# A decoder trunk on one core: the first down group's weights prepared block by block, the statistics' transpose in another PSUM bank, and the merge's low parts on Pool

## The chip, the cores and the metric

The kernel runs on one core of a Trainium2 chip. Its engines work side by side, each through its own queue of instructions in a fixed order: TensorE (PE in the profile) does the matrix products, with a weight load (PEld) ahead of each matmul; VectorE (DVE) and ScalarE (ACT) do elementwise work; GpSimd (POOL) does a little of it; SyncE (SP) issues the DMAs. Matmul results land in PSUM, all other tiles lie in SBUF. An engine waits at an instruction until the semaphores it needs have been raised, and what is queued behind it waits too.

The metric is device time in microseconds, the median over several executions.

## The reference

Two layers of a decoder trunk on 1024 tokens of width 1024, then a last RMSNorm. In each layer:

```
h = rmsnorm(x, norm1)
proj = h @ w_in                      # q, k, v of two mixers, and two gates
o_a = dilated_mixture(...)           # 3 groups x 4 heads, sliding windows, combined by their softmax denominators
o_b = stick_breaking_attention(...)  # 4 heads
merged = sigmoid(gate_a) * (o_a @ w_br[:256]) + sigmoid(gate_b) * (o_b @ w_br[256:])
x = x + merged @ w_o
up = rmsnorm(x, norm2) @ w_up        # 2 x 2816 columns: a gate half and a value half
a = causal_depthwise_conv(a, conv_w, conv_b)   # 3 taps
x = x + (gelu(a) * v) @ w_down
```

All inputs and outputs are float32.

## The kernel before, in words

**Products.** A float32 product is made of three matmuls in a reduced format: every operand is split into a high part `hi` (a cast) and a low part `lo` (the difference), and hi x hi, hi x lo and lo x hi are summed in PSUM. The helper `split` does it: ACT casts (L141), DVE subtracts (L148). `piece` does the same into a ring of four weight slots (tags `wh` and `wl`). One tile is 128 partitions x 512 columns, and most elementwise instructions handle one tile.

**Seven products.** The up chunks and the down-projection use a scheme of the Strassen kind: a product of 2 x 2 blocks is made of seven block products, each of which takes a sum or difference of weight blocks, made on DVE, and of inputs, and adds into one or more outputs.

**The up stage.** An up chunk (`up(j)`) is one unit of a chain. A unit's work is emitted in pieces; at its beginning and at each of its "turns" (five in an up chunk) the next unit is moved on by one piece, so that it can load and prepare its first weights while this one still multiplies. The convolution of a chunk (ACT L1468, DVE L1470 and L1471, ACT's Gelu L1473) and its gating (L1496) come after its last products. The gated result `g` is split, written to DRAM as `gd`, and read back as `gd_in` for the down-projection.

**The down stage.** `down(box)` is the last unit of the chain. It has 28 steps: four groups (of 2, 2, 3 and 4 row blocks of w_down) times the seven products k = 0 to 6. Step s multiplies one weight tile per row block i (two of them in the first group) with `gd_in`, into four PSUM banks e = 0 to 3 (L1759 to L1761, each block 3 matmuls per bank), and adds each bank to x on DVE (L1767). Steps 0 to 3 of a group use the same four banks, so the first matmul of s=1 in bank e waits for the add of bank e from s=0. `prep` prepares the weights of a step: for k=0 the difference a11 - a21 into `wd_s` (L1730, needed later) and the split of a11; for k=1 a sum in place (L1733), a difference in place (L1734) and the split; for k=6 a difference in place (L1737). In the last up chunk's turns, the unit loads the two raw blocks (`wd_raw`) and the inputs of two steps, and at the fifth turn calls `prep(0, 1)`: the weights of s=0, block 0 and then block 1. Those of s=1 are prepared by `prep(0)` when the down stage itself begins.

**The statistics' transpose.** In the near part of the first mixer, when the last item of a pair of heads has been folded, a 128 x 32 tile of softmax statistics is transposed by PE into a PSUM bank (`st0_t`), copied out by ACT (`st_r`, L842) and written to DRAM. PSUM has eight banks in four tags of two ("t", "o", "s", "ps"); the transpose takes one of tag "t", as do the transposes of the attention weights (`t1`, L921 to L923), whose results ACT and DVE split into `p1h` and `p1l` for the products into `o1` (L931, L933).

**The merge stage.** Sixteen items (two halves n of the tokens, eight column blocks e) a layer. An item is two products on PE into two banks `br_ps` (L182 to L184, 12 matmuls), two multiplications with the gates on DVE (L1416, `gin`), their sum on DVE (L1421, `mrg`), and one item later `merged`: ACT casts the high part `hh` (L1381), DVE subtracts the low part `hl` (L1382). DVE also makes the low parts of the branch weights `br_w` and of the first weights of the output projection here. The output projection (`o_ps`, L182 to L184 too) follows and reads `hh` and `hl` of all eight column blocks.

**What sets the order.** The instructions of each engine are ordered by a scheduler from the order of the code, its own estimates of durations, and priorities: what stands under `tc.high_priority(offset=AHEAD)`, such as the adds of L1767, is treated as if it had been written 200 instructions sooner.

Of the kernel before, what the change touches and what calls it, by code (L numbers as in the profile page):

```python
# [8 lines left out]
F32R = mybir.dt.float32r  # L9
# [3 lines left out]
ALU = mybir.AluOpType  # L13
# [3 lines left out]
P = 128  # L17
# [3 lines left out]
HF = 512  # L21
# [15 lines left out]
READY = 6  # L37
# [19 lines left out]
def f32(ap):  # L57
    return ap.bitcast(F32)
# [3 lines left out]
def trunk_kernel(ctx, tc, x, norm1, w_in, b_gate, w_br, w_o, norm2, w_up, conv_w, conv_b, w_down, norm_f, out, depth=None, probe=None):  # L62
# [62 lines left out]
    def bank(tag, name):  # L125
        return ps.tile([P, 512], F32, tag=tag, name=name)

    def small(name, dtype=F32):
        return sb.tile([P, 512], dtype, tag="pt", bufs=PT, name=name)
# [8 lines left out]
    def split(hi, lo, src, turn=None, behind=None):  # L138


        one = act.copy(hi, src)  # L141
        if behind:
            tc.add_manual_dep(one.ins, behind[0], NO_SYNC, reason="behind")
        if turn == "is":
            LAST["act"] = one.ins.name
        elif turn == "waits" and "act" in LAST:
            tc.add_manual_dep(one.ins, LAST["act"], NO_SYNC, reason="in turn")
        two = dve.tensor_tensor(lo, src, f32(hi), ALU.subtract)  # L148
        if behind:
            tc.add_manual_dep(two.ins, behind[1], NO_SYNC, reason="behind")  # L150
        if turn == "is":
            LAST["dve"] = two.ins.name
        return two
# [622 lines left out]
    def near_item(dense, pr, s):  # L776
        if s == 0:
            R["st0", pr] = sb.tile([P, 2, 2, 8], F32, tag="st0", bufs=2, name="st0")
        if "on" not in R:
            R["on"] = sb.tile([P, 2, T], F32, tag="xa", bufs=4, name="on")  # L780
        slot = 2 * pr + s
        q, kv, on, st = R["slots"], R["kvn", slot], R["on"], R["st0", pr]
        k, v = kv[:, 0, :], kv[:, 1, :]
        got, shared = {}, {}

        def score(m):
            if m == 0:
# [12 lines left out]
            for b, c, zz in todo:  # L800
                pp = got[b // 4][:, 256 * (b % 4) + c : 256 * (b % 4) + 256]
                nm = st[:, 0, s, b : b + 1]
                dve.tensor_tensor_reduce(pp, zz, shared["bias"][:, c:256], 1.0, 3e38, ALU.add, ALU.min, nm)
                act.activation(pp, pp, AF.Exp, bias=nm, scale=-1.0, accum_out=st[:, 1, s, b : b + 1])
            if m == 3:
                dense.near = slot + 1

        def turn(i, some):
            tp = bank("t", "t0")
            w = 0  # L810
            for kb, bs in some:
                for b in bs:
                    col = 256 * (b % 4) + (P if b == kb else 0)
                    pe.transpose(tp[:, w * P : (w + 1) * P], got[b // 4][:, col : col + P], ident)
                    w += 1
            shared[i] = parts(tp, w * P, "p0")

        def apply(i, some, n, first, last):
            if first:
                shared["o"] = bank("o", "o0")  # L820
            o = shared["o"]
            w = 0
            for kb, bs in some:
                c0, nb = (bs[0] - 4 * n) * P, len(bs) * P
                for p in (0, 1):
                    pe.matmul(
                        o[:, c0 : c0 + nb],
                        v[:, kb * P : (kb + 1) * P],
                        shared[i][p][:, w * P : w * P + nb],
                        start=(first and w == 0 and p == 0),  # L830
                        stop=(last and kb == some[-1][0] and p == 1),
                        skip_group_check=True,
                    )
                w += len(bs)
            if last:
                fold(on[64 * s : 64 * s + 64, pr, n * HF : (n + 1) * HF], o)
                if s == 1 and n == 1:
                    tp = bank("t", "st0_t")
                    pe.transpose(tp[0:32, 0:P], st.rearrange("p a s b -> p (a s b)"), ident)
                    row = sb.tile([32, P], F32, tag="pt", bufs=PT, name="st0_r")  # L840
                    with tc.high_priority(offset=AHEAD):
                        act.copy(row, tp[0:32, 0:P])  # L842
                    nc.sync.dma_start(dn[pr].rearrange("c (b p) -> (c b) p", p=P), row)


        micro = []
        for n, sets in enumerate(
            (
                [[(0, [0, 1]), (1, [1, 2])], [(2, [2, 3]), (3, [3])]],
                [[(3, [4]), (4, [4, 5])], [(5, [5, 6]), (6, [6, 7])], [(7, [7])]],  # L850
            )
        ):
            for i, some in enumerate(sets):
                micro.append(
                    (
                        lambda i=(n, i), some=some: turn(i, some),
                        lambda i=(n, i), some=some, n=n, f=(i == 0), la=(i == len(sets) - 1): apply(i, some, n, f, la),
                    )
                )
        return [lambda m=m: score(m) for m in range(4)], micro  # L860
# [414 lines left out]
    def mixer(l, pending):  # L1275
# [103 lines left out]

        def merged(n, e, m):  # L1380
            act.copy(H[n][0][:, e, :], m)  # L1381
            dve.tensor_tensor(H[n][1][:, e, :], m, f32(H[n][0][:, e, :]), ALU.subtract)  # L1382

        wo = [wo_chunk(l, n, e) for n in range(2) for e in range(KD)]

# [55 lines left out]
    def ffn(l, pending, final):  # L1441
# [234 lines left out]
        def down(box):  # L1676
# [31 lines left out]
            def place(s, g):  # L1708

                used = [tag for v in range(s, state["w"] + 1) for tag, _ in ws.get(v, ())]  # L1710
                for tag in ("p4", "w") if g else ("w",):
                    if used.count(tag) < 4:
                        return tag

            def prep(s, most=3):

                while state["w"] < min(s + most, count):
                    v = state["w"]
                    g, k = flat[v]
                    m = GROUPS[g]  # L1720
                    used = [tag for u in range(s, v) for tag, _ in ws[u]]
                    room = 4 - used.count("w") + (4 - used.count("p4") if g else 0)
                    if room < m or (g, m - 1) not in raws:
                        return
                    ws[v] = []
                    for i in range(m):
                        a11, a12, a21, a22 = raws[g, i]
                        if k == 0:
                            temps[i] = small("wd_s")
                            dve.tensor_tensor(temps[i], a11, a21, ALU.subtract)  # L1730
                            src = a11
                        elif k == 1:
                            dve.tensor_tensor(a21, a21, a22, ALU.add)  # L1733
                            dve.tensor_tensor(a11, a21, a11, ALU.subtract)  # L1734
                            src = a11
                        elif k == 6:
                            dve.tensor_tensor(a11, a12, a11, ALU.subtract)  # L1737
                            src = a11
                        else:
                            src = {2: temps[i], 3: a22, 4: a12, 5: a21}[k]  # L1740
                        tag = place(s, g)
                        if tag == "p4":
                            w = sb.tile([P, 2, HF], F32R, tag="p4", bufs=4, name="wd")
                            w = (w[:, 0, :], w[:, 1, :])
                            split(*w, src)
                        else:
                            w = piece(src)
                        ws[v].append((tag, w))
                    state["w"] += 1

            def product_of(s, e, sub=slice(0, HF)):
# [23 lines left out]
            load_raw(0, 1, "e8")  # L1775
            load_g()
            load_g()
            for _ in range(READY - 3):
                yield
            prep(0, 1)  # L1780
            yield
            yield
            for s, (g, k) in enumerate(flat):
                while state["g"] < count and state["g"] <= s + (3 if flat[state["g"]][0] else 2):
                    load_g()
# [358 lines left out]
```

## Time and profile before

| what | value |
|---|---|
| time, median of 3 runs | 2637.95 us (2636.91 to 2640.12) |
| the profiled execution's own time | 2637.43 us |
| its span, first to last instruction | 2635.7 us |
| its mean granted TensorE clock | 0.997 |
| PE busy | 2611.4 us (99%) |
| DVE busy | 2091.1 us (79%) |
| ACT busy | 1358.0 us (52%) |
| POOL busy | 55.1 us (2%), all in the attention stages and at the start |

A row of a timeline gives the start and the duration in us, the engine, the line, the operation, what it writes and reads, the shape, and in brackets how long the engine had been idle before it and which instruction the profile takes to have released it. Where several semaphores are waited for, that is the one that came last by the profile, and it can be the wrong one. Durations of one engine overlap a little: a 128x512 DVE operation lasts 0.69 us, and the next starts 0.60 us after it. A row of waits gives the total, the number of times and the longest. A row of a tile gives durations in ns (least, median, most), and the first and the last start.

### The profile page before, as it was taken

The page shows a single profiled execution, that of the slowest core. Times are in us where ns is not written, and L with a number is a line of the kernel's source. Part 1 is how long each engine was busy: PE and PEld are TensorE (multiplying, and loading weights), DVE is VectorE, ACT ScalarE, POOL GpSimd, SP SyncE. Part 2 cuts the span into 40 slices and gives each one's busy share as a digit, 9 for nine tenths or more (in the row PEclk, how much of TensorE's full clock was granted, in tenths as well). Part 3 has the DMA queues.
Part 4 walks back from the last instruction along what each step waited for, and adds up shares of the span by engine and source line. Part 5 has one row for each costly group of instructions (what it writes and reads, how often), then busy time and mean ns, then how long its engine had stood idle before and what let it go on. Part 6 is the DMA issues. An engine that isn't in the chain of part 4 may idle for free.

```text
span 2635.7 us, 36161 instructions
## 1 busy us (share of the span) xinstructions
PE 2611.4 (99%) x12732; PEld 2187.5 (83%) x12732; DVE 2091.1 (79%) x3517; ACT 1358.0 (52%) x2533; POOL 55.1 (2%) x103
## 2 busy tenths in 40 slices
PE   9999999999999999999999999999999999999999
PEld 8888888888888888788888888888888888887888
DVE  8878777795988888897677788777869888888865
ACT  6555666663554545422445555666645545454225
POOL 3000000000000000000000000000000000000000
PEclk9999999999999999999999999999999999999999
DMA  7434578873244454697344436797633354447863
GB/s 254 150 118 136 163 205 216 214 231 101 88 149 155 144 168 144 238 331 285 144 145 144 128 123 190 197 232 210 201 97 120 120 175 139 158 144 275 339 221 115
DMA packets 400417, 468.22 MB, mean 178 GB/s; under 512 B 24308, under 2 KB 315500, under 8 KB 398444
## 3 DMA queue, kind: packets, MB, share of 16 engines
q1 hardware_dynamic: 400220, 465.90, 55.0%
q8 instruction: 101, 1.65, 0.3%
q14 instruction: 80, 0.66, 0.1%
q10 hardware_dynamic: 16, 0.00, 0.0%
HBM read 303.23 MB, written 162.59 MB: 177 GB/s over the span
## 4 chain that ended last, share of the span: by engine, by line
PE 94%; DVE 3%; ACT 2%; issue 1%; DMA 1%; SPq 0%; POOL 0%; DVEq 0%; ACTq 0%; POOLq 0%
PE u_a L1014 5%; PE u_a L1016 5%; PE u_a L1015 5%; PE d_ps L1759 5%; PE d_ps L1761 5%; PE d_ps L1760 5%; PE i_a L1014 5%; PE i_a L1016 5%; PE i_a L1015 5%; PE u_c L1014 3%; PE u_c L1016 3%; PE u_c L1015 3%; PE i_c L1014 2%; PE i_c L1016 2%; PE i_c L1015 2%; PE o_ps L182 2%
## 5 line engine op out<-in xcount | busy, mean ns | idle before, releaser
L141 ACT CAST w_hi<-up_a 128x512 fp32r<-128x512 f32 x280 | 174.1, 622 | 277.3 <-DVE up_a L1617 120.6
L148 DVE TENSOR_TENSOR w_lo<-up_a,w_hi 128x512 fp32r<-128x512 f32 x280 | 189.5, 689 | 83.4 <-ACT w_hi L141 83.4
L141 ACT CAST w_hi<-in_a 128x512 fp32r<-128x512 f32 x252 | 156.2, 622 | 162.2 <-PE i_c L1015 37.3
L148 DVE TENSOR_TENSOR w_lo<-in_a,w_hi 128x512 fp32r<-128x512 f32 x252 | 173.0, 688 | 74.4 <-ACT w_hi L141 64.6
L1767 DVE TENSOR_TENSOR x<-x,d_ps 128x512 f32<-128x512 f32 (+1 forms) x228 | 154.0, 675 | 70.8 <-PE d_ps L1761 68.6
L1759 PE MATMUL d_ps<-gd_in,w_hi 128*128 128x512 f32 (+1 forms) x340 | 131.9, 388 | 10.6 <-ACT g L141 10.6
L1760 PE MATMUL d_ps<-gd_in,w_hi 128*128 128x512 f32 (+1 forms) x340 | 131.4, 387 | 0.0
L1761 PE MATMUL d_ps<-gd_in,w_lo 128*128 128x512 f32 (+1 forms) x340 | 131.3, 386 | 0.0
L1014 PE MATMUL u_a<-hh,w_hi 128*128 128x512 f32 x320 | 124.5, 389 | 0.0
L1015 PE MATMUL u_a<-hl,w_hi 128*128 128x512 f32 x320 | 124.5, 389 | 0.0
L1016 PE MATMUL u_a<-hh,w_lo 128*128 128x512 f32 x320 | 124.5, 389 | 0.0
L1014 PE MATMUL u_a<-t_hi,w_hi 128*128 128x512 f32 x320 | 124.5, 389 | 0.0
L1015 PE MATMUL u_a<-t_lo,w_hi 128*128 128x512 f32 x320 | 124.5, 389 | 0.0
L1016 PE MATMUL u_a<-t_hi,w_lo 128*128 128x512 f32 x320 | 124.5, 389 | 0.0
L1014 PE MATMUL i_a<-hh,w_hi 128*128 128x512 f32 x288 | 119.1, 414 | 0.0
L1014 PE MATMUL i_a<-t_hi,w_hi 128*128 128x512 f32 x288 | 118.3, 411 | 0.0
L1759 PE MATMUL d_ps<-gd_in,wd 128*128 128x512 f32 (+1 forms) x292 | 113.9, 390 | 0.0
L1016 PE MATMUL i_a<-hh,w_lo 128*128 128x512 f32 x288 | 113.2, 393 | 0.0
L1016 PE MATMUL i_a<-t_hi,w_lo 128*128 128x512 f32 x288 | 113.0, 392 | 0.0
L1015 PE MATMUL i_a<-t_lo,w_hi 128*128 128x512 f32 x288 | 112.8, 392 | 0.0
L1761 PE MATMUL d_ps<-gd_in,wd 128*128 128x512 f32 (+1 forms) x292 | 112.8, 386 | 0.0
L1015 PE MATMUL i_a<-hl,w_hi 128*128 128x512 f32 x288 | 112.8, 392 | 0.0
(379 smaller groups left out, 7801.1 us busy)
## 6 DMA issues: line engine op xcount, KB each, us to landing
gd<-g SPq DMA_DIRECT2D x154, 512.0 KB, 3.9
gd_in<-gd SPq DMA_DIRECT2D x154, 512.0 KB, 5.8
up_a<-in_w_up_dram SPq DMA_DIRECT2D x80, 512.0 KB, 5.0
in_a<-in_w_in_dram SPq DMA_DIRECT2D x72, 512.0 KB, 4.9
wd_raw<-in_w_down_dram SPq DMA_DIRECT2D x22, 1024.0 KB, 7.9
gin<-gs SPq DMA_DIRECT2D x32, 512.0 KB, 4.2
w_raw<-in_w_o_dram SPq DMA_DIRECT2D x64, 256.0 KB, 2.9
gs<-u SPq DMA_DIRECT2D x48, 256.0 KB, 4.1
```

The source lines that it names most:

```text
L141: one = act.copy(hi, src)
L148: two = dve.tensor_tensor(lo, src, f32(hi), ALU.subtract)
L182: pe.matmul(o, lh, rh, start=(first and i == 0), stop=False, skip_group_check=share)
L1014: pe.matmul(o, w[0][:, c], rh, start=(first and i == 0), stop=False, skip_group_check=True)
L1015: pe.matmul(o, w[0][:, c], rl, start=False, stop=False, skip_group_check=True)
L1016: pe.matmul(o, w[1][:, c], rh, start=False, stop=(last and i == 3), skip_group_check=True)
L1759: pe.matmul(o[:, sub], wh[:, c], gh[:, sub], start=(i == 0 and k in (0, 4, 5)), stop=False, skip_group_check=True)
L1760: pe.matmul(o[:, sub], wh[:, c], gl[:, sub], start=False, stop=False, skip_group_check=True)
L1761: pe.matmul(o[:, sub], wl[:, c], gh[:, sub], start=False, stop=(i == m - 1), skip_group_check=True)
L1767: dve.tensor_tensor(x, x, o[:, sub], ALU.add)
```

## The change

It has three parts.

1. `prep` in the down stage is taken apart: its body for one row block i of one step v becomes `prep_one(s, v, i)`. In the last up chunk's turns the unit now prepares one block per turn, in the order (step 0, block 0), (step 1, block 0), (step 0, block 1), and (step 1, block 1) at the end, before its own steps begin. Before, it prepared step 0 with both blocks at the fifth turn, and step 1 with both blocks in the first step.
2. `st0_t` takes a bank of tag "o" instead of "t".
3. The low part of `merged` is subtracted by Pool instead of DVE, 16 times a layer.

```diff
@@ near part of the first mixer @@
                 if s == 1 and n == 1:
-                    tp = bank("t", "st0_t")
+                    tp = bank("o", "st0_t")
@@ merge stage @@
         def merged(n, e, m):
             act.copy(H[n][0][:, e, :], m)
-            dve.tensor_tensor(H[n][1][:, e, :], m, f32(H[n][0][:, e, :]), ALU.subtract)
+            pool.tensor_tensor(H[n][1][:, e, :], m, f32(H[n][0][:, e, :]), ALU.subtract)
@@ down(box) @@
+            def prep_one(s, v, i):
+
+                g, k = flat[v]
+                a11, a12, a21, a22 = raws[g, i]
+                if k == 0:
+                    temps[i] = small("wd_s")
+                    dve.tensor_tensor(temps[i], a11, a21, ALU.subtract)
+                    src = a11
+                elif k == 1:
+                    dve.tensor_tensor(a21, a21, a22, ALU.add)
+                    dve.tensor_tensor(a11, a21, a11, ALU.subtract)
+                    src = a11
...
+                ws.setdefault(v, []).append((tag, w))
+
             def prep(s, most=3):
...
-                    ws[v] = []
                     for i in range(m):
...
-                        ws[v].append((tag, w))
+                        prep_one(s, v, i)
                     state["w"] += 1
...
             load_raw(0, 1, "e8")
             load_g()
             load_g()
-            for _ in range(READY - 3):
+            yield
+            for v, i in ((0, 0), (1, 0), (0, 1)):
+                prep_one(0, v, i)
                 yield
-            prep(0, 1)
-            yield
-            yield
+            for _ in range(READY - 5):
+                yield
+            prep_one(0, 1, 1)
+            state["w"] = 2
             for s, (g, k) in enumerate(flat):
```

PE's order is the same before and after; what differs there is what it waits for. At the statistics' transpose PE has before (in brackets the engine whose semaphore the row waits for):

```order
L921 MATMUL t1_4615<-ident_66,p1_4513 128x128
L922 MATMUL t1_4615<-ident_66,p1_4513 128x128
L923 MATMUL t1_4615<-ident_66,p1_4513 128x128
L921 MATMUL t1_4623<-ident_66,p1_4513 128x128 [waits Activation_49]
L922 MATMUL t1_4623<-ident_66,p1_4513 128x128
L923 MATMUL t1_4623<-ident_66,p1_4513 128x128
```

and after the same rows:

```order
L921 MATMUL t1_4615<-ident_66,p1_4513 128x128
L922 MATMUL t1_4615<-ident_66,p1_4513 128x128
L923 MATMUL t1_4615<-ident_66,p1_4513 128x128
L921 MATMUL t1_4623<-ident_66,p1_4513 128x128
L922 MATMUL t1_4623<-ident_66,p1_4513 128x128
L923 MATMUL t1_4623<-ident_66,p1_4513 128x128
```

The second group of transposes no longer waits for ACT. DVE, ACT and POOL differ in the merge stage and at the passage from the last up chunk to the down stage, in both layers; the rows here are those of layer 1. The numbers behind names count tiles: `d_ps_10567` to `d_ps_10570` are the banks e = 0 to 3 of steps 0 to 3, `wd_raw_10403` and `wd_raw_10471` the raw blocks 0 and 1, `u_10409` and `cv_10593` belong to the last up chunk.

DVE at that passage, before, from a sum of the last up chunk on:

```order
L1654 TENSOR_TENSOR u_10409<-u_10409,u_b_10514 128x512
L1730 TENSOR_TENSOR wd_s_10528<-wd_raw_10403 128x512
L148 TENSOR_TENSOR w_lo_10531<-wd_raw_10403,w_hi_10530 128x512
L1730 TENSOR_TENSOR wd_s_10534<-wd_raw_10471 128x512
L148 TENSOR_TENSOR w_lo_10537<-wd_raw_10471,w_hi_10536 128x512
L1733 TENSOR_TENSOR wd_raw_10403<-wd_raw_10403 128x512
L1470 TENSOR_SCALAR cv_10593<-u_10409,cw_83,cv_10593 128x1023
```

The weights of both blocks for s=0 follow L1654 here. Five rows further on, DVE goes on with the third and then, after six other operations, the fourth add of step 0:

```order
L1767 TENSOR_TENSOR x0_6058<-x0_6058,d_ps_10570 128x512
L1733 TENSOR_TENSOR wd_raw_10471<-wd_raw_10471 128x512
L1496 TENSOR_TENSOR cv_10593<-cv_10593,u5_10410 128x512
L1734 TENSOR_TENSOR wd_raw_10471<-wd_raw_10471 128x512
L1496 TENSOR_TENSOR cv_10593<-cv_10593,u_a_10411 128x512
L1737 TENSOR_TENSOR wd_raw_10403<-wd_raw_10403 128x512
L148 TENSOR_TENSOR w_lo_10564<-wd_raw_10471,w_hi_10563 128x512
L1767 TENSOR_TENSOR x0_6058<-x0_6058,d_ps_10567 128x512
```

Bank e = 0 is the last of the four here. The same place after the change (L1654 has kept its number; L1730, L1733, L1734 and L1767 are now L1721, L1724, L1725 and L1771):

```order
L1725 TENSOR_TENSOR wd_raw_10403<-wd_raw_10403 128x512
L148 TENSOR_TENSOR w_lo_10523<-wd_raw_10403,w_hi_10522 128x512
L1654 TENSOR_TENSOR u_10409<-u_10409,u_b_10526 128x512
L1721 TENSOR_TENSOR wd_s_10540<-wd_raw_10471 128x512
L148 TENSOR_TENSOR w_lo_10543<-wd_raw_10471,w_hi_10542 128x512
L1724 TENSOR_TENSOR wd_raw_10471<-wd_raw_10471 128x512
L1470 TENSOR_SCALAR cv_10593<-u_10409,cw_83,cv_10593 128x1023
L1725 TENSOR_TENSOR wd_raw_10471<-wd_raw_10471 128x512
L1471 TENSOR_SCALAR cv_10593<-u_10409,cw_83,cv_10593 128x1022
L1771 TENSOR_TENSOR x0_6058<-x0_6058,d_ps_10568 128x512
L148 TENSOR_TENSOR w_lo_10561<-wd_raw_10471,w_hi_10560 128x512
L1771 TENSOR_TENSOR x0_6058<-x0_6058,d_ps_10567 128x512
```

The work on block 0 has moved ahead of L1654, the gating (L1496) and L1737 behind the adds, and the add of `d_ps_10567` from the fourth to the second place among the adds of step 0.

DVE in the middle of the merge stage, before:

```order
L1416 TENSOR_TENSOR gin_6130<-gin_6130,br_ps_6199 128x512
L1382 TENSOR_TENSOR hl1_5996<-mrg_6157,hh1_5995 128x512
L1421 TENSOR_TENSOR mrg_6207<-gin_6130 128x512
L1416 TENSOR_TENSOR gin_6161<-gin_6161,br_ps_6217 128x512
L1382 TENSOR_TENSOR hl1_5996<-mrg_6183,hh1_5995 128x512
L1416 TENSOR_TENSOR gin_6161<-gin_6161,br_ps_6225 128x512
L1382 TENSOR_TENSOR hl0_5978<-mrg_6207,hh0_5977 128x512
L1416 TENSOR_TENSOR gin_6187<-gin_6187,br_ps_6248 128x512
L1421 TENSOR_TENSOR mrg_6233<-gin_6161 128x512
L1416 TENSOR_TENSOR gin_6187<-gin_6187,br_ps_6256 128x512
L148 TENSOR_TENSOR br_w_6241<-br_raw_6242,br_w_6241 128x512
```

Here the low parts (L1382) stand between the products with the gates. The same place after the change:

```order
L148 TENSOR_TENSOR w_lo_6323<-w_raw_6320,w_hi_6322 128x512
L1421 TENSOR_TENSOR mrg_6183<-gin_6104 128x512
L1416 TENSOR_TENSOR gin_6130<-gin_6130,br_ps_6191 128x512
L148 TENSOR_TENSOR br_w_6241<-br_raw_6242,br_w_6241 128x512
L1416 TENSOR_TENSOR gin_6130<-gin_6130,br_ps_6199 128x512
L148 TENSOR_TENSOR br_w_6241<-br_raw_6242,br_w_6241 128x512
L1416 TENSOR_TENSOR gin_6161<-gin_6161,br_ps_6217 128x512
L1421 TENSOR_TENSOR mrg_6207<-gin_6130 128x512
L1416 TENSOR_TENSOR gin_6161<-gin_6161,br_ps_6225 128x512
L148 TENSOR_TENSOR w_lo_6329<-w_raw_6326,w_hi_6328 128x512
L1416 TENSOR_TENSOR gin_6187<-gin_6187,br_ps_6248 128x512
L1421 TENSOR_TENSOR mrg_6233<-gin_6161 128x512
```

The L1382 rows are gone from DVE, and the splits of the weights (`br_w`, `w_lo`) stand one to two items sooner. The subtractions stand in Pool's queue, where nothing was at this place:

```order
L870 MEMSET t_kq 64x2x256 x2
L1382 TENSOR_TENSOR hl_5978<-mrg,hh_5977 128x512 x2
L1382 TENSOR_TENSOR hl_5996<-mrg,hh_5995 128x512 x2
L1382 TENSOR_TENSOR hl_5978<-mrg,hh_5977 128x512 x2
L1382 TENSOR_TENSOR hl_5996<-mrg,hh_5995 128x512 x2
L1382 TENSOR_TENSOR hl_5978<-mrg,hh_5977 128x512 x2
```

They follow the clearing of two tiles of the attention stage, and in layer 1 come ahead of the next layer's `slots`.

More of the change, by code (lines that the diff above doesn't have):

```diff
@@ L1713, in place @@
                         return tag
+            def prep_one(s, v, i):
[9 more added lines that the diff above has]
+                    src = a11
+                elif k == 6:
+                    dve.tensor_tensor(a11, a12, a11, ALU.subtract)
+                    src = a11
+                else:
+                    src = {2: temps[i], 3: a22, 4: a12, 5: a21}[k]
+                tag = place(s, g)
+                if tag == "p4":
+                    w = sb.tile([P, 2, HF], F32R, tag="p4", bufs=4, name="wd")
+                    w = (w[:, 0, :], w[:, 1, :])
+                    split(*w, src)
+                else:
+                    w = piece(src)
+                ws.setdefault(v, []).append((tag, w))
             def prep(s, most=3):
@@ L1724, in prep @@
                         return
-                    ws[v] = []
                     for i in range(m):
[L1727 to L1747, printed above, removed]
-                        ws[v].append((tag, w))
+                        prep_one(s, v, i)
                     state["w"] += 1
```

## The prediction

> **What bounds the kernel now.** I read the page first (busy time, share of the span and instructions of each engine):
>
> ```profile
> PE 2611.4 (99%) x12732; PEld 2187.5 (83%) x12732; DVE 2091.1 (79%) x3517; ACT 1358.0 (52%) x2533; POOL 55.1 (2%) x103
> ```
>
> TensorE (PE) works 2611.4 of 2635.7 us, and the change adds and removes no matmul. So the time can fall only where PE stands still or is clocked down, and rise only where it is made to wait. The view of PE's waits names where it stands (in all, times, longest):
>
> ```profile
> PE d_ps L1759 <- ACT g L141: 10.6, 2, 5.3
> PE t L921 <- ACT st_r L842: 2.3, 2, 1.2
> PE warm L2034 <- POOL ident masks.py:199: 1.8, 1, 1.8
> PE br_ps L184 <- DVE br_w L148: 1.1, 2, 0.6
> ```
>
> Each twice is once per layer. The first is the passage from the last up chunk to the down-projection, the second the statistics' transpose, the fourth the merge stage: the change touches all three. The first costs more than its 5.30 us. The timeline of PE there, layer 1 and then layer 2:
>
> ```profile
> 1103.74 0.39 PE L1761 MATMUL d_ps<-gd_in,w_lo 128*128 128x512 f32 x1
> ...
> 1106.46 0.39 PE L1761 MATMUL d_ps<-gd_in,w_lo 128*128 128x512 f32 x1
> 1112.15 0.77 PE L1759 MATMUL d_ps<-gd_in,w_hi 128*128 128x512 f32 x1 [5.30 <-ACT g L141]
> ...
> 1118.30 0.39 PE L1759 MATMUL d_ps<-gd_in,w_hi 128*128 128x512 f32 x1
> ```
>
> ```profile
> 2408.81 0.39 PE L1761 MATMUL d_ps<-gd_in,w_lo 128*128 128x512 f32 x1
> 2414.51 0.77 PE L1759 MATMUL d_ps<-gd_in,w_hi 128*128 128x512 f32 x1 [5.30 <-ACT g L141]
> ...
> 2419.79 0.40 PE L1759 MATMUL d_ps<-gd_in,w_hi 128*128 128x512 f32 x1
> ```
>
> Twelve matmuls run from 1103.74 to 1106.46, a pitch of 2.72 / 12 = 0.2267 us. After the wait a matmul itself is slower, 0.77 for 0.39. The windows (PE, PEld, DVE, ACT, POOL busy, then the granted clock) say why:
>
> ```profile
> 1110.00:1115.00 5.00, 2.85 (x7) 2.32 (x8) 5.00 (x10) 3.02 (x6) 0.00 (x0) 0.60 0.63 252
> 1140.00:1150.00 10.00, 10.00 (x45) 8.28 (x45) 9.86 (x18) 3.00 (x5) 0.00 (x0) 1.00 1.03 415
> ```
>
> The clock granted was 0.60 there, and 1.00 later. [...] In rows alone: the matmul at 1118.30 is the 16th after 1106.46, and at full pitch it would stand at 1106.46 + 16 x 0.2267 = 1110.09. So this passage costs 8.21 us in layer 1; in layer 2, 2419.79 - (2408.81 + 3.63) = 7.35. Together **15.56 us**.
>
> **Part 1, the weights block by block.** The view blames ACT's `g`, but the matmul at 1112.15 opens step s=1 in the PSUM bank that step s=0 has just filled, and must wait until DVE has added that bank to x. DVE's timeline, with ACT's `g` and the cast that waited for the second raw block:
>
> ```profile
> 1098.73 0.69 DVE L1654 TENSOR_TENSOR u<-u,u_b 128x512 f32<-128x512 f32 x1 [2.03 <-PE u_b L1016]
> 1099.33 0.69 DVE L1730 TENSOR_TENSOR wd_s<-wd_raw 128x512 f32<-128x512 f32 x1
> ...
> 1102.34 1.28 DVE L1470 SCALAR_TENSOR_TENSOR cv<-u,cw,cv 128x1023 f32<-128x1023 f32 x1
> 1103.54 0.69 DVE L1734 TENSOR_TENSOR wd_raw<-wd_raw 128x512 f32<-128x512 f32 x1
> ...
> 1111.37 0.69 DVE L1767 TENSOR_TENSOR x<-x,d_ps 128x512 f32<-128x512 f32 x1
> ```
>
> ```profile
> 1097.83 0.62 ACT L141 CAST w_hi<-wd_raw 128x512 fp32r<-128x512 f32 x1 [2.87 <-DMA wd_raw<-in_w_down_dram]
> ...
> 1111.31 0.61 ACT L141 CAST g<-cv 128x512 fp32r<-128x512 f32 x1
> ```
>
> The fourth add of s=0 runs at 1111.37 to 1112.06 and PE starts at 1112.15. It is bank e=0 that comes last, behind the other three and behind operations on the weights of s=1 that the scheduler put ahead of it. DVE is not idle in between (5.00 of 5 from 1110 to 1115); the order is the wait.
>
> After the change five DVE operations (the difference and low part of block 0 for s=0; its sum, difference and low part for s=1) stand ahead of L1654, under the up chunk, where DVE was idle 2.03 us right before L1654 alone. Behind L1654 the new order has nine starts to the add of bank e=0: L1654, difference, low part, sum, L1470, second difference, L1471, the add of bank 1, a low part, and then that add. At the trace's pitch of 0.60 for a 128x512 operation and 1.20 for L1470 and L1471 that is 7 x 0.60 + 2 x 1.20 = 6.6 us. From 1098.73 the add starts at 1105.33 and ends at 1106.02. PE is due with s=1 at 1106.46 + 0.23 = 1106.69. If L1654 is held by the low part now ahead of it, by at most one 0.69, it ends at 1106.71. With handoffs of 0.09 (1112.06 to 1112.15) the rest of the wait is 0 to 0.7; I take 0.3 per layer. The cast of block 1 for s=0 still waits for its load (landed just before 1097.83) and isn't moved past it. The part moves no DMA: SP's queue is the same, and POOL's has nothing here. ACT's extra cast ahead is 0.62 in a stretch with 2.87 idle. Gain: 15.56 - 0.6 = **14.96**; ends 15.56, and 10 if 2.5 us per layer stay, without a clock drop.
>
> **Part 2, another bank for the transpose.** PE, ACT and DVE at this place:
>
> ```profile
> 421.10 0.27 PE L923 MATMUL t<-ident,p 128*128 128x128 f32 x1
> 422.54 0.33 PE L921 MATMUL t<-ident,p 128*128 128x128 f32 x1 [1.16 <-ACT st_r L842]
> ...
> 424.43 0.28 PE L931 MATMUL o<-p1l,slots 128*128 128x256 f32 x1
> ```
>
> ```profile
> 422.23 0.26 ACT L842 COPY st_r<-st_t 32x128 f32<-32x128 f32 x1
> 423.14 0.56 DVE L148 TENSOR_TENSOR p1l<-t,p1h 128x384 fp32r<-128x384 f32 x1
> ```
>
> The second L921 needed the "t" bank that st_r frees at 422.49. From an "o" bank the transpose holds no "t", and L921 follows at 421.10 + 0.11 = 421.21: 1.33 earlier. Then L931 on p1l is due at 424.43 - 1.33 = 423.10, but p1l comes from DVE, behind its own queue, at 423.70, and with the handoff of 0.09 PE waits 0.69 there. Net 0.64 per layer, **1.28** in all. Ends: 0, if p1l slips by as much as was won, and 2.66.
>
> **Part 3, the low part of merged on Pool.** The merge stage is 16 items a layer, on PE 12 matmuls = 2.72 us each. The group of its DVE sum, then from the start of the run the nearest rows of Pool and of DVE beside it, then PE's first matmul of the output projection:
>
> ```profile
> L1421 DVE TENSOR_TENSOR mrg<-gin x32: 684/688/698, 548.8 to 1891.3; 128x512 f32<-128x512 f32 x32
> ```
>
> ```profile
> 29.82 0.61 POOL L170 CAST kq_w<-w_raw 128x512 fp32r<-128x512 f32 x1 [5.39 <-DMA w_raw<-in_w_in_dram]
> 30.51 1.30 POOL L171 TENSOR_TENSOR kq_w<-w_raw,kq_w 128x512 fp32r<-128x512 f32 x1
> ```
>
> ```profile
> 29.64 0.68 DVE L581 TENSOR_TENSOR vb<-v_ps,vb 128x512 fp32r<-128x512 f32 x1
> 30.24 0.60 DVE L2012 SCALAR_TENSOR_TENSOR h_raw<-x_part,g,x_rb 128x128 f32<-128x128 f32 x2
> 30.75 1.61 DVE L148 TENSOR_TENSOR hl<-h_raw,hh 128x512 fp32r<-128x512 f32 x1
> ```
>
> ```profile
> 586.58 0.39 PE L182 MATMUL o_ps<-hh,w_hi 128*128 128x512 f32 x1
> ```
>
> DVE loses 0.60 per item, and the `br_w` split that PE waited for is placed earlier: 0.55 per layer off. But Pool needs 1.30 where DVE needed 0.69, and it is not free of DVE: while Pool runs at 30.51 a DVE subtraction of two SBUF tiles takes 1.61 for 0.69 and ends 0.55 after Pool; with one PSUM input, at 29.64 beside Pool's cast, it takes 0.68. [...] `mrg` and the splits have two SBUF inputs, the gate products (gin with br_ps) one.
>
> So a ring forms: mrg 0.69, ACT's cast 0.62 (as at 1097.83), Pool 1.30, three handoffs of 0.09, then the next mrg: 2.88 us against PE's 2.72, 16 x 0.16 = 2.6 us late at the end. Eight weight splits fall in the stage; each can push a mrg by 0.60 and hold Pool by 0.60: 0 to 9.6 us, 4.8 as the middle. Slack: PE takes item 13's low part last in its first output chunk, at 586.58 + 22 x 0.2267 = 591.57; unhindered it would be there at 581.3 (two items before 586.58) + 0.8 (gate product) + 2.88 = 585.0, so 6.6 us. Late by 7.4 less 6.6 is 0.8; and DVE's add of that chunk can stand behind a split that Pool holds, up to 1.3, of which I count half, 0.7. Cost 1.5, range 0 to 5.6 + 1.3; with -0.55, **+0.95 per layer, +1.9 in all** (-1.1 to +12.7). [...]
>
> **Sum.** -14.96 - 1.28 + 1.9 = -14.34 against the profiled execution's 2637.43 us (span 2635.7): 2623.1. The median of the runs shown is 2637.95, 0.5 above it; with the same step **2623.6 us**.
>
> **Rivals.**
> (a) DVE becomes the bound of the down stage. At 1140 to 1150 it is busy 9.86 of 10, and PE, no longer held for 8 us, asks for the same adds 8 us sooner. With five operations (3.0 us) done earlier, up to 5 us per layer (8 - 3) can come back as short waits in s=1 to s=5, 1 to 5 in each layer: 2626 to 2634, middle 2630. Against it: a bank's add isn't due before PE is back at that bank, a step of 24 matmuls or 5.44 us later, so that DVE may lag by several operations before PE waits.
> (b) The ring costs 4 to 6 us per layer rather than 1.5: 2637.95 - 16.24 - 1.1 + 8 to 12, 2629 to 2633. For it: every term of the slip at its upper end.
> (c) The other side: each mrg and each split waits for a whole Pool operation. An item then takes three DVE starts 1.80, half a split 0.30, Pool 1.30 on each mrg and 0.65 for half a split: 4.05 against 2.72, 21.3 us late after 16 items, less 6.6 slack = 14.7 per layer. With -0.55 that is +28.3 in all, against -16.2 from the other parts: 2650. It decides from a late end of 6.6 + 8.1 + 0.55 = 15.25 us, that is 0.95 an item, or an item of 3.67 us. [...]
> (d) Part 1 does not do what it says: ACT's `g`, as the view has it, or the load holds s=1, and the stall stays: about 2637. Against it: `g` is not an input of s=1's first matmul, and ended at 1111.92, 0.23 before it.
>
> **How the numbers follow.** Chances: the forecast 0.66 (own range 2619 to 2628: everything at its best is 2637.95 - 15.56 - 2.66 - 1.1 = 2618.6), (a) 0.14, (b) 0.11, (c) 0.05, (d) 0.04. The range 2619 to 2632 holds the forecast, most of (a) and most of (b). About 0.2%, 5.3 us, is what a measurement of this kernel can tell from none: below 2632.7 lie the forecast, 0.12 of (a), 0.10 of (b), so faster 0.88; same 0.06 (the rest of (a) and (b), and 0.03 of (d)); slower 0.06 ((c), and 0.01 of (d)).
>
> **What would show it.** Right: the wait of L1759 for `g` is gone or under 1 us, no window near 1106 has a granted clock under 0.9, the fourth add of s=0 ends before 1106.8; L921 no longer waits for st_r, and a wait of about 0.7 for p1l stands in its place; Pool shows 32 more subtractions of about 1.3 with mrg rows of up to 2 us beside them, and PE waits for `hl` at most some 2 us per layer. Wrong: short PE waits for DVE's adds behind 1112 (a), waits of 4 us or more at o_ps (b, c), or an untouched 5.30 (d).

## The result, and the profile after

The changed kernel takes 2621.91 us (median of 6 runs, 2620.94 to 2622.79), the kernel before 2638.05 us beside it (6 runs): a ratio of 0.9938, 95% interval 0.9925 to 0.995, or 16.1 us. Forecast were 2623.6 us, in a range of 2619 to 2632. The profiled execution took 2621.54 us, its span is 2619.8.

The page's first part and the first waits of PE, of the kernel after:

```profile
PE 2606.3 (99%) x12732; PEld 2185.4 (83%) x12732; DVE 2089.1 (80%) x3485; ACT 1358.8 (52%) x2533; POOL 100.4 (4%) x135
```

```profile
PE z L644 <- DMA t_kq<-tk: 1.8, 2, 1.5
PE warm L2041 <- POOL ident masks.py:199: 1.8, 1, 1.8
PE o L931 <- DVE p1l L148: 1.3, 4, 0.5
```

The three waits that the prediction spoke of (10.6, 2.3 and 1.1 us) are gone. Two have come: for `p1l`, as forecast, and at L644 for loads of `t_kq`, which wasn't. None is for `hl`, the merge's low part on Pool.

At the passage to the down stage (PE, then DVE, then the windows, layer 1):

```profile
1104.99 0.39 PE L1765 MATMUL d_ps<-gd_in,w_lo 128*128 128x512 f32 x1
1105.27 0.51 PE L1763 MATMUL d_ps<-gd_in,w_hi 128*128 128x512 f32 x1
1105.61 0.40 PE L1764 MATMUL d_ps<-gd_in,w_hi 128*128 128x512 f32 x1
```

```profile
1097.93 0.68 DVE L1654 TENSOR_TENSOR u<-u,u_b 128x512 f32<-128x512 f32 x1
...
1104.53 1.88 DVE L1771 TENSOR_TENSOR x<-x,d_ps 128x512 f32<-128x512 f32 x3
```

```profile
1105.00:1110.00 5.00, 5.00 (x23) 3.89 (x22) 4.83 (x9) 0.76 (x2) 0.00 (x0) 1.00 1.02 410
```

Step 1 opens at 1105.27, 0.28 behind the matmul before it where the pitch is 0.23. The add of bank e = 0 is the first of the three from 1104.53, 6.60 us after L1654, as counted. The clock granted is 1.00.

PE's order is the same in both kernels, so the starts of its 12732 matmuls can be compared one by one. How much earlier PE is after the change, and what each stretch gave:

| at (time in the kernel before) | PE earlier by | this stretch | what lies in it |
|---|---|---|---|
| 400 | 0.64 | -0.64 | the start; the run on the order alone, alike up to layer 1's down stage, is 0.67 ahead of before at L1654 |
| 432 | 1.24 | -0.60 | transposes, layer 1 |
| 447 | 0.58 | +0.66 | waits for t_kq |
| 580 | 1.42 | -0.84 | merge, layer 1 |
| 1106 | 1.47 | -0.05 | |
| 1125 | 9.46 | -7.99 | up to down, layer 1 |
| 1700 | 9.35 | +0.11 | |
| 1733 | 9.94 | -0.59 | transposes, layer 2 |
| 1737 | 8.40 | +1.54 | wait for t_kq |
| 1890 | 9.24 | -0.84 | merge, layer 2 |
| 2408 | 8.94 | +0.30 | |
| 2425 | 16.09 | -7.15 | up to down, layer 2 |

The passage gave 15.14 us and the merge stages 1.7. The transposes gave 1.2, and 2.2 were lost again at the next loads of `t_kq`.

### The profile page after: what moved, and what is told of

It reads as the page before. It is cut to its first block, busy times and chain, and to the rows that moved or that the text cites. A ratio compares the mean times of both kernels' runs of the same rounds, so it can differ in the third digit from the quotient of the medians.

```text
span 2619.8 us, 36195 instructions
## 1 busy us (share of the span) xinstructions
PE 2606.3 (99%) x12732; PEld 2185.4 (83%) x12732; DVE 2089.1 (80%) x3485; ACT 1358.8 (52%) x2533; POOL 100.4 (4%) x135
## 4 chain that ended last, share of the span: by engine, by line
PE 94%; DVE 2%; ACT 2%; DMA 1%; issue 1%; SPq 0%; POOL 0%; DVEq 0%; ACTq 0%; POOLq 0%
PE u_a L1014 6%; PE u_a L1016 6%; PE u_a L1015 6%; PE d_ps L1763 5%; PE d_ps L1764 5%; PE d_ps L1765 5%; PE i_a L1014 5%; PE i_a L1016 4%; PE i_a L1015 4%; PE u_c L1014 3%; PE u_c L1016 3%; PE u_c L1015 3%; PE i_c L1014 2%; PE i_c L1016 2%; PE i_c L1015 2%; PE o_ps L182 2%
## 5 line engine op out<-in xcount | busy, mean ns | idle before, releaser
L1771 DVE TENSOR_TENSOR x<-x,d_ps 128x512 f32<-128x512 f32 (+1 forms) x228 | 153.8, 676 | 64.9 <-PE d_ps L1765 61.5
L1763 PE MATMUL d_ps<-gd_in,wd 128*128 128x512 f32 (+1 forms) x292 | 114.0, 390 | 0.0
L1765 PE MATMUL d_ps<-gd_in,wd 128*128 128x512 f32 (+1 forms) x292 | 112.9, 387 | 0.0
L1764 PE MATMUL d_ps<-gd_in,wd 128*128 128x512 f32 (+1 forms) x292 | 112.9, 387 | 0.0
```

The lines of the kernel that those rows point to most:

```text
L1763: pe.matmul(o[:, sub], wh[:, c], gh[:, sub], start=(i == 0 and k in (0, 4, 5)), stop=False, skip_group_check=True)
L1764: pe.matmul(o[:, sub], wh[:, c], gl[:, sub], start=False, stop=False, skip_group_check=True)
L1765: pe.matmul(o[:, sub], wl[:, c], gh[:, sub], start=False, stop=(i == m - 1), skip_group_check=True)
L1771: dve.tensor_tensor(x, x, o[:, sub], ALU.add)
```

## The experiments

**One part at a time.** The first kernel has part 1 alone, the second the transpose's bank alone, the third Pool's subtraction alone, the fourth all but that; each is put together from the diff's parts. Where a single run is given, it is read by its trace: the nine runs of the kernel before that stand beside these lie between 2636.94 and 2640.38, so that a difference of a us or two says little by itself.

> Part 1 alone: the weights of the first down group block by block, the transpose and the merge as before. Theory (the parts are independent and part 1 carries the result): both 5.30 us waits of L1759 vanish with the slow stretch behind them, about 0.1 us per layer is left, so about 15 us faster than before (2623). Rival (Pool's subtraction in the merge stage is what gave part of the gain, by taking DVE work away): clearly less, 12 us or below.

Measured: 2622.23 us (5 runs, 2621.57 to 2622.41), ratio 0.994 (0.9927 to 0.9952). The whole result, within a us. The passage gave 7.99 and 7.18 us.

> Part 2 alone: the transpose in an o bank. Theory from the trace after the change (PE gains 1.3 us per layer at L921, gives 0.65 back at p1l, and then catches up with the loads of t_kq, which don't come sooner): the wait for st_r is gone, a wait for p1l of about 0.5 us and waits for t_kq of 0.3 to 1.5 us stand in its place, net 0.5 us faster to 1 us slower in all. Forecast of the prediction: 1.3 us faster in all, no wait for t_kq.

Measured: 2637.8 us in one run, against a median of 2638.21 before. PE's waits in this kernel:

```profile
PE d_ps L1759 <- ACT g L141: 10.6, 2, 5.3
PE warm L2034 <- POOL ident masks.py:199: 1.8, 1, 1.8
PE br_ps L184 <- DVE br_w L148: 1.6, 3, 0.6
PE o L931 <- DVE p1l L148: 1.3, 4, 0.5
```

The wait for `st_r` is gone, and PE gains 0.58 and 0.56 us at the transposes of the two layers. Nothing of that is left soon after: 0.9 us are given back in the merge stage of layer 1, at a longer wait for `br_w`, and 0.8 in layer 2 at L644, where the view names the load of `slots` and not, as expected, that of `t_kq`. Part 2 by itself is worth nothing that shows.

> Part 3 alone: merged's low parts on Pool. Theory (the ring of sum, cast and subtraction runs late but inside the slack of 6.6 us, so PE never waits for it, and the wait for br_w goes): 1.3 us faster in all, no wait of PE at o_ps. Forecast of the prediction: PE waits about 1.5 us per layer at o_ps, 1.9 us slower in all.

Measured: 2635.39 us in one run. No wait at `o_ps` or for `br_w` is left, and PE gains 0.81 us in the first merge stage and 0.90 in the second: 1.7 us, where the prediction had a cost of 1.9.

> Parts 1 and 2, the merge's low parts on DVE as before. Theory: the changed kernel without the 1.3 us that part 3 gave: about 1.3 us slower than the changed kernel, 14 to 15 us faster than before, with the two br_w waits of 0.55 us back. Forecast of the prediction: about 2 us faster than the changed kernel, since no ring forms.

Measured: 2622.78 us (5 runs, 2621.37 to 2624.95). That is about a us above the changed kernel, but the two sets of runs overlap. The traces say more: PE gains nothing in the two merge stages here (0.04 and -0.12 us against before), where the changed kernel gains 0.84 in each. The forecast that leaving part 3 out would win 2 us is wrong.

**The same without part 2.**

> Parts 1 and 3 without part 2. Theory (part 2 is worth nothing, since PE gives its gain back at p1l and at the loads of t_kq): the same time as the changed kernel within 1 us, 2621 to 2623. Forecast of the prediction: 1.3 us slower than the changed kernel.

Measured: 2621.62 us (5 runs, 2620.55 to 2622.74), 0.3 us below the changed kernel: part 2 adds nothing to parts 1 and 3. Its trace against the changed one's says where part 2 goes: without it the second L921 comes 1.32 us later in both layers, 0.66 us are regained at p1l, and at the next `t_kq` the rest is, in layer 2 even 0.6 us more.

**What gives part 2's gain back.** SyncE's queue in the changed kernel, from the last keys written to the loads of the item behind the transpose (layer 2):

```profile
1715.11 0.54 SPq L1211 DMA_DIRECT2D tk<-last  x1
1715.74 0.60 SPq L843 DMA_DIRECT2D dn<-st_r  x1
1716.43 1.59 SPq L1128 DMA_DIRECT2D in_a<-in_w_in_dram  x2
1718.08 1.86 SPq L874 DMA_DIRECT2D t_kq<-tk  x2
```

```profile
1725.86 0.30 PE L644 MATMUL z<-t_kq 128*128 128x128 f32 x1 [1.50 <-DMA t_kq<-tk]
```

The loads are issued right behind two loads of weights, and PE's matmul that reads them starts 6 us after the second is issued. In the kernel before, PE already came there with nothing to spare, since its matmul stood 0.36 behind the last one, at a pitch of 0.23:

```profile
1733.91 0.39 PE L1016 MATMUL i_c<-hh,w_lo 128*128 128x512 f32 x1
1734.27 0.30 PE L644 MATMUL z<-t_kq 128*128 128x128 f32 x1
```

The next kernel gives all loads of `t_kq` a higher place, not these alone; the orders of PE, DVE and ACT are those of the changed kernel.

```diff
-        nc.sync.dma_start(f32(t[0:64]), there[:, :, 1:4, :])
+        with tc.high_priority(offset=60): nc.sync.dma_start(f32(t[0:64]), there[:, :, 1:4, :])
         for g in range(2):
-            nc.sync.dma_start(f32(t[64:128, g, 0:2, :]), there[:, g, 0:3:2, :])
+            with tc.high_priority(offset=60): nc.sync.dma_start(f32(t[64:128, g, 0:2, :]), there[:, g, 0:3:2, :])
```

> The changed kernel with the loads of t_kq given a higher place in SyncE's queue (the orders of PE, DVE and ACT are the same), so that those for the item behind the transpose are issued ahead of the writes of the last keys and of the two loads of weights instead of behind them. Theory (PE gives part 2's gain back because these loads land too late, not for some other reason): PE's waits for t_kq of 0.3 and 1.5 us are gone or under 0.2, the gain of part 2 stays, and the time is 1 to 2 us below the changed kernel (2620 to 2621). Rival (the loads are bound by the DMA engines or by the keys written before them, not by their place in the queue; or something else holds PE there): the waits stay, or stand at another load, 2621 to 2623.

Measured: 2619.58 us (5 runs, 2619.13 to 2621.03), ratio to before 0.9934 (0.992 to 0.9948). Against the changed kernel PE is 0.55 us earlier at the first of the two places and 1.77 at the second, and the wait for `t_kq` no longer stands in the view:

```profile
PE warm L2041 <- POOL ident masks.py:199: 1.8, 1, 1.8
PE o L931 <- DVE p1l L148: 1.3, 4, 0.5
PE sb_t L746 <- DVE beta L738: 0.9, 2, 0.5
```

The place in SyncE's queue was the cause. PE even passes the second place 0.2 us faster than in the kernel before, so that there, too, it had been waiting a little. This version has the lowest median of all that ran, below both kernels; its interval overlaps that of the changed kernel, so that the 2.3 us between the two rest on the traces.

**Order or work.** The prediction said that the add of bank e = 0 was late by its place in DVE's order. The next kernel is the one before with `prep(0)` called behind the products of step 0; nothing is prepared in the up chunk that wasn't before.

```diff
-                prep(s)
+                if s:
+                    prep(s)
...
                 for e in range(4):
                     for _ in product_of(s, e):
                         pass
...
                     yield
+                if s == 0:
+                    prep(0)
```

> The kernel before, with one thing moved: the weights of step 1 are asked for after the products of step 0 instead of ahead of them, so that the add of bank e = 0 no longer stands behind them on DVE; nothing is prepared earlier, block by block or otherwise. Theory (the place of that add in DVE's order is the wait, as the prediction says): counted along DVE's new order at 0.60 and 1.20 us a start, the add ends at about 1103.7 and the last low part of step 1 at about 1107.5, when PE needs it, so the stall falls to 0 to 0.6 us per layer and the time is 14 to 16 us below before (2622 to 2624), as with part 1. Rival (there is too much work on DVE between the two steps, and only what is moved under the up chunk helps): PE starts step 1 but then waits 3 us or more for the weights of block 1, 2628 or more.

Measured: 2628.11 us (5 runs, 2627.71 to 2629.78), ratio 0.9965 (0.9951 to 0.9978). Neither the theory's 2622 to 2624 nor the rival's wait at step 1. The add of bank e = 0 now runs first, and ACT's `g` later (DVE, then ACT, layer 1):

```profile
1102.28 0.68 DVE L1767 TENSOR_TENSOR x<-x,d_ps 128x512 f32<-128x512 f32 x1
```

```profile
1118.74 0.62 ACT L141 CAST g<-cv 128x512 fp32r<-128x512 f32 x1 [1.19 <-DVE cv L1496]
```

Step 1 opens at 1106.02 without a wait, 12.7 us ahead of that `g`, and both waits of 5.30 with their slow stretches are gone: PE gains 8.2 us between 1106 and 1125, and 7.4 up to 2425. But then it gives 3.4 and 3.2 us back, in short waits for low parts of weights:

```profile
PE d_ps L1761 <- DVE w_lo L148: 2.7, 6, 1.0
PE t L921 <- ACT st_r L842: 2.3, 2, 1.2
PE warm L2037 <- POOL ident masks.py:199: 1.8, 1, 1.8
PE sb_t L746 <- DVE beta L738: 0.9, 2, 0.5
PE br_ps L184 <- DVE br_w L148: 0.8, 2, 0.5
PE d_ps L1761 <- DVE wd L148: 0.8, 2, 0.4
```

That is close to the prediction's rival (a), DVE as the bound of the down stage, in a kernel that changes the order alone; only that PE waits for weights here and not for adds. So part 1 does two things: it brings the add forward, which ends the stall, and it moves five DVE operations per layer into idle time under the up chunk, without which 6.6 us of the 15.6 come back later.

**A shorter stall.** The changed kernel, with both blocks of step 1 at the end of the up chunk:

```diff
-            for v, i in ((0, 0), (1, 0), (0, 1)):
+            yield
+            for v, i in ((0, 0), (0, 1)):
                 prep_one(0, v, i)
                 yield
             for _ in range(READY - 5):
                 yield
+            prep_one(0, 1, 0)
             prep_one(0, 1, 1)
```

> The changed kernel, but both blocks of step 1 prepared at the end of the last up chunk instead of block 0 two turns earlier: half the dose of part 1. Counted along DVE's order the add of bank e = 0 starts 13 x 0.60 + 2 x 1.20 = 10.2 us after L1654, where the changed kernel has 6.6, so PE waits 3.0 to 3.7 us per layer at the first matmul of step 1. [...]

Measured: 2630.23 us (7 runs, 2628.34 to 2632.18), 8.3 above the changed kernel. PE waits 2.91 us in each layer, a little under the count of 3.0 to 3.7, and the add of bank e = 0 ends right before. In the profiled execution the clock stayed up behind the first wait and fell behind the second (windows of layer 1, then of layer 2; the second figure is PE's busy time, the seventh the granted clock):

```profile
1104.25:1107.66 3.41, 1.48 (x7) 0.90 (x5) 3.41 (x7) 1.43 (x3) 0.00 (x0) 1.00 1.03 420
1107.66:1111.08 3.42, 2.44 (x11) 2.03 (x12) 3.42 (x7) 0.84 (x2) 0.00 (x0) 1.00 1.01 405
2404.73:2408.14 3.41, 1.18 (x5) 1.03 (x6) 3.41 (x7) 1.48 (x3) 0.00 (x0) 1.00 1.02 408
2408.14:2411.56 3.42, 3.42 (x9) 2.66 (x9) 1.92 (x4) 1.24 (x2) 0.00 (x0) 0.50 0.51 200
```

> The same kernel as in the run with both blocks of step 1 at the end, once more. There PE waited 2.91 us in each layer and the clock fell behind one of the two waits only, for 3.4 us. [...] Rival (something in layer 2 alone makes it fall): fallen in layer 2 alone again.

Measured: 2630.22 us in one run, and this time the clock fell in both layers, at the same waits of 2.91 us; in layer 1 it fell while PE still waited:

```profile
1104.08:1107.49 3.41, 1.08 (x5) 0.56 (x3) 3.41 (x7) 1.66 (x3) 0.00 (x0) 1.00 1.03 417
1107.49:1110.90 3.41, 2.83 (x7) 2.30 (x8) 2.28 (x4) 0.62 (x1) 0.00 (x0) 0.50 1.02 410
2404.56:2407.97 3.41, 0.52 (x2) 0.48 (x3) 3.41 (x7) 1.66 (x3) 0.00 (x0) 1.00 1.02 413
```

It is not tied to the layer. In the down stages of the kernel before, the granted clock changed at 1110.98, 1117.81, 2411.46 and 2418.29, whose distances are 2, 379 and 2 times 3.413 us. The two falls of this run, at 1107.49 and 2407.97, lie 381 times that apart, and the windows above are cut in the same steps. Ahead of the three falls PE was idle for 2.23 (3.41 less 1.18 busy), 2.33 and 2.89 us of such an interval. The wait that brought no fall was shared between two intervals, with 1.93 us of idle time in the one and 0.98 in the other. So what differed was where the wait lay in these intervals, and that differed from run to run. At the second wait of 5.30 in the kernel before, too, PE was busy for 1.15 us of the interval ahead of the fall:

```profile
2408.05:2411.46 3.41, 1.15 (x6) 0.61 (x4) 3.41 (x7) 1.06 (x1) 0.00 (x0) 1.00 1.03 417
2411.46:2414.88 3.42, 0.38 (x1) 0.41 (x2) 3.42 (x6) 2.18 (x4) 0.00 (x0) 0.50 1.01 406
```

Matmul by matmul against the changed kernel, a wait of 2.91 costs 2.97 us without a fall and 4.28, 4.57 and 4.58 with one, so that the fall, 3.41 us at a clock of 0.50, cost 1.3 to 1.6.

**Pool's price doubled.** The subtraction of `merged` is issued twice in a row, with the same result; all else is the changed kernel.

```diff
-            pool.tensor_tensor(H[n][1][:, e, :], m, f32(H[n][0][:, e, :]), ALU.subtract)
+            pool.tensor_tensor(H[n][1][:, e, :], m, f32(H[n][0][:, e, :]), ALU.subtract); pool.tensor_tensor(H[n][1][:, e, :], m, f32(H[n][0][:, e, :]), ALU.subtract)
```

> The changed kernel with each of merged's Pool subtractions done twice in a row. Theory (sum, cast and subtraction form a ring, since DVE's sum has two SBUF inputs and can't run beside Pool's subtraction): an item takes 0.69 + 0.62 + 2.6 + 0.27 = 4.2 us against PE's 2.72, so the stage is 23 us late or more at its end, less 6.6 us of slack: 17 us or more of waits per layer, 2655 or later. Rival (no ring: DVE and Pool run side by side, and Pool's 2.6 us per item is under 2.72): no wait to speak of, under 2625.

Measured: 2637.56 us in one run, 16 above the changed kernel: between the two forecasts. PE's waits, and the merge's sum and subtraction:

```profile
PE o_ps L183 <- POOL hl L1382: 6.9, 4, 2.0
PE o_ps L182 <- DVE gin L1416: 3.1, 2, 1.6
```

```profile
L1382 POOL TENSOR_TENSOR hl<-mrg,hh x64: 1270/1624/1847, 550.5 to 1902.4; 128x512 fp32r<-128x512 f32 x64
L1421 DVE TENSOR_TENSOR mrg<-gin x32: 691/1450/1785, 548.9 to 1898.3; 128x512 f32<-128x512 f32 x32
```

```profile
550.47 35.79 POOL L1382 TENSOR_TENSOR hl<-mrg,hh 128x512 fp32r<-128x512 f32 x22 [129.96 <-ACT hh L1381]
```

Pool runs through, 22 subtractions in 35.79 us, or 3.25 us for the two of an item, where the ring would have had 4.2 for an item. Both are slower beside each other (a median of 1.62 us for 1.30 on Pool, 1.45 for 0.69 on DVE), but no sum took more than 1.79, where the two subtractions of an item took 3.25: none waited for both. PE waited 5 us per layer, and in layer 1 the clock fell at two waits that were 1 us apart, of 1.47 and 1.95 us:

```profile
593.54 0.50 PE L183 MATMUL o_ps<-hl,w_hi 128*128 128x512 f32 x1 [1.47 <-POOL hl L1382]
...
596.46 0.74 PE L183 MATMUL o_ps<-hl,w_hi 128*128 128x512 f32 x1 [1.95 <-POOL hl L1382]
596.99 0.63 PE L184 MATMUL o_ps<-hh,w_lo 128*128 128x512 f32 x1
```

```profile
593.13:596.55 3.42, 1.05 (x4) 0.58 (x4) 3.23 (x4) 1.22 (x2) 3.34 (x4) 1.00 0.00 0
```

The end of the first wait and the whole of the second lie in one interval of 3.41 us, in which PE was busy for 1.05 only; from 596.00 to 600.00 the clock was 0.57, and matmuls of 0.39 us took 0.63.

## Why the prediction was right, and which of its terms weren't

**Part 1: forecast 14.96, measured 15.14** (7.99 and 7.15), and 15.2 with part 1 alone. The start of the add, counted along the new order, was 6.6 us after L1654 and is 6.60. The 0.3 us per layer taken for the rest of the wait was 0.05 at the first matmul of layer 1, and 0.2 over the whole passage (15.56 - 15.14 for both layers). That the view's releaser was not the real one held: in the experiment on the order the stall went with the add, while `g` came 7.4 us later than before. Incomplete was "the order is the wait": without the work taken ahead, 3.2 to 3.4 us per layer come back, much like rival (a).

**Part 2: forecast -1.28, measured +1.0.** L921 came 1.3 us sooner and p1l took 0.65 of it, both as worked out. The step that failed is the end of that sum: it stopped at p1l and did not ask what PE meets next. That was a load whose issue hung on SyncE's queue and not on PE. The row before would have shown it, a matmul at L644 0.36 behind its neighbour. Some 0.3 us of the 1.54 lost there in layer 2 aren't part 2's: the kernel without it loses them too. Against that kernel part 2 costs 0.6 us.

**Part 3: forecast +1.9, measured -1.7.** What the prediction read from one row is there: beside Pool, `mrg` with its two SBUF inputs lengthens (a median of 0.88 us and up to 1.78, for 0.69 before), the products with a PSUM input don't (0.67 to 0.69). The groups of the changed kernel's first merge stage:

```profile
L1421 DVE TENSOR_TENSOR mrg<-gin x16: 679/884/1784, 548.1 to 590.0; 128x512 f32<-128x512 f32 x16
```

```profile
L1416 DVE TENSOR_TENSOR gin<-gin,br_ps x32: 673/676/694, 545.0 to 589.2; 128x512 f32<-128x512 f32 x32
```

Mis-sized were three terms. The ring was put at 2.88 us, of which mrg and a handoff made 0.78 and the other two handoffs 0.18. In the trace a mrg that starts beside a running subtraction of Pool's ends 0.55 us behind it, and the two handoffs take 0.03 and 0.08, so that the ring closes in 0.55 + 0.03 + 0.62 + 0.08 + 1.29 = 2.57. Three of its sums start 2.58 and 2.57 apart, under PE's 2.72:

```profile
581.75 1.28 DVE L1421 TENSOR_TENSOR mrg<-gin 128x512 f32<-128x512 f32 x1
582.96 1.27 DVE L1416 TENSOR_TENSOR gin<-gin,br_ps 128x512 f32<-128x512 f32 x2
584.33 1.27 DVE L1421 TENSOR_TENSOR mrg<-gin 128x512 f32<-128x512 f32 x1
585.53 1.27 DVE L1416 TENSOR_TENSOR gin<-gin,br_ps 128x512 f32<-128x512 f32 x2
586.90 1.78 DVE L1421 TENSOR_TENSOR mrg<-gin 128x512 f32<-128x512 f32 x1
```

The next sum starts 3.08 later, although no split comes between: ACT was busy with another operation, and Pool's subtraction started half a us late. Over the stage the 16 sums from 548.1 to 590.0 stand 2.79 us apart on average, so that the loop does fall behind PE, but by about 1 us, and not by the 2.6 of the ring and the 4.8 of the splits, the second term. Item 13's low part was ready at 586.85 + 1.29 = 588.14 and taken by PE at 590.14. That is 4.5 us late by the prediction's count (585.0, less the 1.4 us by which PE was earlier), not 7.4, and 2.0 us of the slack were left. The doubled subtraction shows how near this is: at twice Pool's time PE waits about 5 us per layer. The third term is the wait for `br_w`, counted at the 0.55 us of the view; the stage gained 0.84. A matmul of 0.39 us is followed by the next after 0.23, so that a wait costs about 0.16 more than the idle time shown, and the matmul behind it is slower as well (0.77 for 0.39): the wait of 5.30 made its matmul 5.46 late.

The errors of parts 2 and 3, +2.3 and -3.6, and 0.6 us at the start, nearly cancel by luck: both parts came out with the other sign. So the sum lay only 1.7 us above what was measured. Its weight lay in part 1, and there the mechanism was right. Of the rivals, something like (a) happens where only the order is changed, (b) and (c) did not come, and (d) fell with the stall.

**The clock.** The 15.56 us hold the slow stretches behind the two waits, and the lower end of part 1's gain, 10 us, leaves waits of 2.5 us per layer in place without such a stretch. No run shows that term. In the changed kernel 0.05 of the wait was left in layer 1, and the granted clock was 1.00 from 1105 to 1110. Of four waits of 2.91 us three brought a fall, and so did two of 1.47 and 1.95 close together, where PE had been idle for 2.23 to 2.89 us of the 3.41 ahead of the fall.

## What to carry to other kernels

Where a view blames a wait on the last semaphore, follow the bank or the buffer instead: count the instructions ahead of its release on the engine that releases it, before and after; here that count gave the gain of part 1 within 0.2 us. Then count on to the weights behind it: where the order alone was changed, 6.6 us came back there. A removed stall is worth only what the next meeting point leaves of it, so follow PE to the next load whose issue doesn't depend on PE, and read in the old trace how much that load had to spare. And work moved to Pool was free here although DVE's sums beside it took up to 1.78 us for 0.69: the loop through both stayed near PE's own time for the item (2.79 on average for 2.72) and its lag, 4.5 us, within the slack of 6.6 before PE needs the result.

## What the runs showed of the hardware

- In the down stages of the kernel before, the granted clock changed at four points, 2, 379 and 2 times 3.413 us apart; the two falls of the second run with both blocks at the end lie 381 times that apart. In the 3.41 us ahead of six falls PE had been idle for 3.41 and 2.26 us (the kernel before), 2.23, 2.33 and 2.89 (both blocks at the end) and 2.37 (the doubled subtraction). Intervals with 1.93 and 0.98 us of idle time, the two parts of one wait of 2.91, were followed by none.
- The clock was at 0.50 for 3.41 us in the two falls behind which PE was idle for 0 and 0.58 us of the next interval (both blocks at the end, layer 2 of the first run and layer 1 of the second), and for 6.83 in the kernel before, where it was idle for 1.17 and 3.04. A fall cost 1.3 to 1.6 us at a wait of 2.91, and at the waits of 5.30 in the kernel before 8.21 - 5.46 = 2.75 and 7.35 - 5.47 = 1.9 us (5.46 and 5.47 being what the first matmul came late).
- In the changed kernel's first merge stage the seven sums from 569.78 on that start beside a running Pool subtraction end 0.54 or 0.55 us behind it, after up to 1.78 us for 0.69. With Pool's subtractions doubled, the median subtraction took 1.62 us for 1.30 and the median sum 1.45 for 0.69.
